# Differential-attention scores on two row halves of TensorE, with a smaller PSUM ring

## The chip, the core and the metric

The kernel runs on one core of a Trainium2 chip. The metric is device time in microseconds (us) of one execution of the whole kernel; lower is better. The engines named below are TensorE (PE; its weight loads are listed apart as PEld), VectorE (DVE), ScalarE (ACT), GpSimd (POOL) and SyncE (SP, which issues most DMAs).

## The reference, cut to what matters

One layer of a diffusion trunk: a SwiGLU feed-forward, then token mixing (differential attention beside a bidirectional mLSTM), then a second feed-forward, each behind a modulated normalization. 512 latent tokens read themselves and 256 cached context keys; 128 prompt tokens read only themselves. The change lies in the attention:

```
scale = DA_HEAD_DIM ** -0.5                      # 64 features, 8 heads, 2 components
def block(qi):                                   # 128 queries
    s = jnp.einsum('bqhcd,bkhcd->bhcqk', qi, kf) * scale
    pr = jax.nn.softmax(s, axis=-1)
    w = pr[:, :, 0] - lam * pr[:, :, 1]
    return jnp.einsum('bhqk,bkhv->bqhv', w, vf)
```

So each head has two components of 64 features; each has its own scores and its own softmax, and the two weight matrices are subtracted before they meet the values.

## The kernel before, in words

**Precision by parts.** Most products are made from numbers split into a high part that the fp32r format holds (a ScalarE copy) and the rest (a VectorE subtraction). A product is the sum of high x high, high x low and low x high (`mm3`).

**Stages.** First the modulation, with products on four column quarters of the array (`product`, line 905, `tile_position=(0, q)`) between the first feed-forward's products; then that feed-forward. Then the attention's pools open at line 1346: `ps2`, a ring of five one-bank PSUM tiles, and `ps2s`, one three-bank tile for scores. In these pools run:

- the first projections (lines 1833 to 1850): `tok_group` makes query tokens 0 and 1, then key tokens 0 and 1 of the first head pair, then query tokens 2, 3, 4, then key tokens 2, 3, 4. Each group takes one bank per token tile of 128, and `norm2(psum, 1)`, called inside the first group, takes one for the norm's sums. ScalarE copies a finished bank into `q_tok` or `k_tok`. The gates' small products go into the score tile (`ps_g`);
- the branch gates (`Gates`, line 1793), with accumulators from `ps2`;
- the attention, head by head, mixed with projection units for later heads and for the mLSTM (`Fill`).

**One head.** `pack_queries` writes per token and component the high part, the low part, the low part and the high part of the other component in four slots of 64; `pack_keys` writes each component's high part twice. `queries`, `keys(0)` and `keys(1)` turn these through TensorE (ten 128x128 transposes each, names `qpk`, `kpk`, `kp`) into tiles with features on the rows: `qT` has for each component its high part on one half of the rows and its low part on the other, `kH` has the high keys twice, `kL` the low keys twice. So one 128-row product of `qT` with `kH` adds high x high and low x high, and one with `kL` adds the rest and low x low. The cached keys come doubled from memory (`cache_kd`).

`scores(qi)` makes for each component 768 columns of scores, in blocks of 512 and 256 that keep inside a PSUM bank: eight matmuls into the three-bank tile. For the prompt's queries (`qi` = 4) four matmuls of 256 columns stand in two banks. VectorE takes a minimum over both components, ScalarE makes two exponentials with sums (`soft`), VectorE mixes them (`mix`), TensorE turns the weights (`turn`, up to six 128x128 transposes, read by ScalarE) and multiplies by the values (`values`, f32, names `ps_o`).

**The order.** TensorE's and SP's instructions keep the order of the code. Inside `with written()` VectorE's and ScalarE's do too; elsewhere a scheduler places them. For each query block the code writes scores, the turning of the block before, exponentials, one projection unit, the mix, the values of the block before, and a second unit where the table `UNITS` (line 1930) says so; heads 6 and 7 have one unit per block, and the queries of head 7 are prepared with no unit between. A unit is 24 matmuls: `ps_t` (token rows, 256 columns) or `ps_p` (feature rows, 320 columns). `gate_rows` (line 1366) is a long chain of small VectorE steps that the scheduler lays between the first head's preparations.

Of the kernel before, what the change touches and what calls it, by code (L numbers as in the profile page):

```python
# [31 lines left out]
def tile_trunk(ctx: ExitStack, tc: tile.TileContext, a: dict):  # L32
    nc = tc.nc
    vec = nc.vector
# [15 lines left out]
    def act(*args, **kw):  # L50
        return placed(nc.scalar.activation(*args, **kw))  # L51

    def tt(eng, out, in0, in1, op):
        return placed(eng.tensor_tensor(out=out, in0=in0, in1=in1, op=op))  # L54
# [19 lines left out]
    def mm(*args, **kw):  # L74
        tc.keep_in_program_order(nc.tensor.matmul(*args, **kw))  # L75
# [32 lines left out]
    ntmp = right.enter_context(tc.tile_pool(name="ntmp", bufs=1, side="right"))  # L108
# [721 lines left out]
    with ExitStack() as ph:  # L830
        fp = ph.enter_context(tc.tile_pool(name="ffn1", bufs=1))
        psum = Banks(ph.enter_context(tc.tile_pool(name="ps1", bufs=1, space=PSUM)))
# [7 lines left out]
        hs = HalfStep(1, fp, ntmp, psum, a["w1a"], a["w3a"], a["w2a"], range(*FIRST_GROUPS[1]))  # L840
# [130 lines left out]
        start = Opening()  # L971
# [371 lines left out]

    att = ExitStack()
    qk = att.enter_context(tc.tile_pool(name="qk", bufs=1))
    psum = att.enter_context(tc.tile_pool(name="ps2", bufs=5, space=PSUM))
    ps_s = att.enter_context(tc.tile_pool(name="ps2s", bufs=1, space=PSUM))

    fill = Fill()
# [2 lines left out]
    def gate_products():  # L1352
        raw = load(rawp, [128, KT, 128], a["w_g"], tag="raw", name="wg_raw")
        wgH = wide_p.tile([128, KT, 128], F32R, tag="BH", name="wgH", bufs=2)
        wgL = wide_p.tile([128, KT, 128], F32R, tag="BL", name="wgL", bufs=2)
        act(wgH, raw, AF.Copy)
        tt(vec, wgL, raw, wgH.bitcast(F32), ALU.subtract)
        ps = ps_s.tile([128, 1536], F32, tag="sc", name="ps_g")

        def step(hf, k):  # L1360
            cs = half(hf)
            mm3(ps[:, 512 * hf : 512 * hf + HALF], wgH[:, k, :], wgL[:, k, :], hH[:, k, cs], hL[:, k, cs], k == 0, k == KT - 1)

        return ps, step
# [125 lines left out]
    q_tok, k_tok, v_tok = {}, {}, {}  # L1490
# [49 lines left out]
    class Head:  # L1540
# [8 lines left out]

        def pack_queries(self):  # L1550

            hs = slice(self.h * 128, (self.h + 1) * 128)
            qv = q_tok[self.pr][:, :, hs].rearrange("p t (c d) -> p t c d", c=2)
            self.qpk = ap.tile([128, 5, 4, 64], F32R, tag="pk", name="qpk", bufs=2)
            act(self.qpk[:, :, 0::3, :], qv, AF.Copy)
            tt(vec, self.qpk[:, :, 1:3, :], qv, self.qpk[:, :, 0::3, :].bitcast(F32), ALU.subtract)

        def pack_keys(self):
            hs = slice(self.h * 128, (self.h + 1) * 128)
            kv = self.kv = k_tok[self.pr][:, :, hs].rearrange("p t (c d) -> p t c d", c=2)  # L1560
            self.kpk = ap.tile([128, 5, 4, 64], F32R, tag="pk", name="kpk", bufs=2)
            for i in range(2):
                self.at_act = act(self.kpk[:, :, i::2, :], kv, AF.Copy)

        def turn_features(self, pk, dst, key, ev):
            for i0, n in ((0, 2), (2, 2), (4, 1)):
# [7 lines left out]

        def queries(self):
            self.qT = ap.tile([128, 2, T], F32R, tag="qT", name="qT")
            self.kH = ap.tile([128, 2, 896], F32R, tag="kH", name="kH")
            self.kL = ap.tile([128, 2, 896], F32R, tag="kL", name="kL")
            self.ao = ap.tile([128, 5, 128], F32, tag="ao", name="ao")
            self.turn_features(self.qpk, self.qT, False, lambda o, i: act(o, i, AF.Copy))  # L1580
            self.kp2 = ap.tile([128, 5, 4, 64], F32R, tag="pk", name="kp2", bufs=2)
            for i in range(2):
                self.at_vec = tt(vec, self.kp2[:, :, i::2, :], self.kv, self.kpk[:, :, i::2, :].bitcast(F32), ALU.subtract)
            ck = load(ap, [128, 2, 256], a["cache_kd"][:, self.hd], tag="asq", name="ck")
            act(self.kH[:, :, 512:768], ck, AF.Copy)
            tt(vec, self.kL[:, :, 512:768], ck, self.kH[:, :, 512:768].bitcast(F32), ALU.subtract)

        def keys(self, part):
            if part == 0:
                self.turn_features(self.kpk, self.kH, True, lambda o, i: vec.tensor_copy(o, i))  # L1590
            else:
                self.turn_features(self.kp2, self.kL, True, lambda o, i: act(o, i, AF.Copy))

        def scores(self, qi):
            s = ps_s.tile([128, 1536], F32, tag="sc", name="sc")
            qs = slice(qi * 128, (qi + 1) * 128)
            qT, kH, kL = self.qT, self.kH, self.kL
            for c in range(2):
                if qi < 4:
                    for k0, k1 in (((0, 512), (512, 768)) if c == 0 else ((0, 256), (256, 768))):  # L1600
                        o = s[:, c * 768 + k0 : c * 768 + k1]
                        mm(o, qT[:, c, qs], kH[:, c, k0:k1], start=True, stop=False)
                        mm(o, qT[:, c, qs], kL[:, c, k0:k1], start=False, stop=True)
                else:

                    o = s[:, c * 512 : c * 512 + 256].rearrange("p (c t) -> p c t", c=2)
                    mm(o, qT[:, c, qs], kH[:, :, 768:896], start=True, stop=False)
                    mm(o, qT[:, c, qs], kL[:, :, 768:896], start=False, stop=True)
            if qi < 4:
                sv = s.rearrange("p (c t) -> p c t", c=2)  # L1610
            else:
                sv = s[:, 0:1280].rearrange("p (c t) -> p c t", c=2)[:, :, 0:128]
            mn, sm, rc = (ap.tile([128, 2], F32, tag=n, name=n, bufs=2) for n in ("mn", "sm", "rc"))
            placed(vec.tensor_reduce(out=mn, in_=sv, axis=AX.X, op=ALU.min))
            self.s[qi] = sv, 768 if qi < 4 else 128, mn, sm, rc
# [201 lines left out]
    ropes, tabs, nlam, gs, rope_p = [], [], [None], [None], [None]  # L1817
    wide = ExitStack()
    wide_p = wide.enter_context(tc.tile_pool(name="wide", bufs=1))
    G = Gates(wide_p, ntmp, psum)  # L1820

    (src_q, e_q), (src_k, e_k) = project_q(0, ropes.append), project_k(0, ropes.append)
    e_q, e_k = e_q(), e_k()
# [11 lines left out]
    with tc.issue_after(box["normed"]):  # L1835
        ps_g, gate_step = gate_products()
# [63 lines left out]
    ap = att.enter_context(tc.tile_pool(name="att", bufs=1, reuse_waits="tile"))  # L1900
# [36 lines left out]
    for hd in range(8):  # L1937
        H = heads[hd]
        odd = hd % 2
        for qi in range(5):  # L1940
            n = UNITS[hd][qi]
# [24 lines left out]
        n = UNITS[hd][-1]  # L1966
# [40 lines left out]
    psum = ml.enter_context(tc.tile_pool(name="ps3", bufs=8, space=PSUM, reuse_waits="tile"))  # L2007
# [238 lines left out]
    psum = Banks(ctx.enter_context(tc.tile_pool(name="ps4", bufs=1, space=PSUM, reuse_waits="tile")))  # L2246
# [67 lines left out]
    hs = HalfStep(2, None, tmp, psum, a["w1b"], a["w3b"], a["w2b"], range(GROUPS[0][0], FB))  # L2314
# [45 lines left out]
    ps = {(f, i): acc_tile(psum) for f in range(2) for i in range(2)}  # L2360
# [9 lines left out]
    ps = {(f, i): acc_tile(psum) for f in range(2) for i in range(2)}  # L2370
# [169 lines left out]
```

## Time and profile before

| what | us |
|---|---|
| median of 3 runs | 1818.51 (1817.56 to 1819.2) |
| span of the profiled execution | 1816.4 |
| TensorE busy in it | 1793.6 (99%) |
| VectorE busy | 1323.8 (73%) |
| ScalarE busy | 894.8 (49%) |

The span runs from the first to the last instruction of the profiled execution; what lies around it (launch and end) is not in it. Matmuls overlap in the timeline: a row's duration runs from its start to its modelled end, and the next matmul begins before that. What a matmul costs in a row of matmuls is therefore the distance between starts. A column with a tile such as 128*128 gives rows and columns of the array that the instruction uses. A bracket at a row's end gives idle time of the engine just before it and what ended it.

### The profile page before, as it was taken

How to read it: one execution, taken by the hardware profiler on the slowest of the kernel's cores; microseconds unless marked ns; L12 is line 12 of the kernel's file. 1: busy time of each engine (PE TensorE's matmuls, PEld its weight loads, DVE VectorE, ACT ScalarE, POOL GpSimd, SP SyncE). 2: the span in 40 equal slices, each digit the busy share in tenths (PEclk: the TensorE clock that was granted, in tenths of full speed). 3: DMA queues.
4: the chain of work that ended last, by engine and by line, in shares of the span. 5: the costliest groups of instructions: out<-in, count | busy, mean ns of one | idle time of the engine just before them, and what ended most of it. 6: DMA issues, size and time to landing. Idle time of an engine off the chain costs nothing.

```text
span 1816.4 us, 30813 instructions
## 1 busy us (share of the span) xinstructions
PE 1793.6 (99%) x12622; PEld 1754.8 (97%) x12622; DVE 1323.8 (73%) x2140; ACT 894.8 (49%) x1558; POOL 37.1 (2%) x65
## 2 busy tenths in 40 slices
PE   9999999999999999999999999999999999999998
PEld 7999999999999999999999889999999999999998
DVE  6889986677886776475575649876767888897485
ACT  5654553333755454455465454674336545554432
POOL 0000000100000000000000000000000000000010
PEclk9999999999999999999999999999999999999999
DMA  8255566977244322112222055665652355657992
GB/s 330 106 197 183 185 224 235 344 228 257 82 138 159 106 76 78 63 63 89 80 89 72 20 169 163 223 254 183 238 170 80 134 172 185 202 181 275 352 307 83
DMA packets 130622, 307.69 MB, mean 169 GB/s; under 512 B 9841, under 2 KB 92017, under 8 KB 117553
## 3 DMA queue, kind: packets, MB, share of 16 engines
q1 hardware_dynamic: 120114, 263.64, 42.1%
q0 software_dynamic: 9680, 39.46, 6.7%
q8 instruction: 99, 1.62, 0.4%
q10 hardware_dynamic: 688, 2.63, 0.4%
q14 instruction: 41, 0.34, 0.1%
HBM read 238.14 MB, written 67.56 MB: 168 GB/s over the span
## 4 chain that ended last, share of the span: by engine, by line
PE 84%; DVE 7%; DMA 5%; ACT 3%; issue 1%; SPq 0%; DVEq 0%; ACTq 0%
PE ps_f L75 43%; PE ps_p L75 19%; PE ps_t L75 11%; PE sc L75 3%; PE ps_o L75 2%; DVE ww L54 2%; PE ps_n L75 2%; DMA raw<-in_w2b 2%; DMA raw_a<-in_w_ada_k 1%; PE ps_wT L78 1%; PE ps_u L75 1%; DVE junk L813 1%; PE ps_qkT L78 1%; DMA out_new_c<-Cn 1%; DMA P<-nm_dram 1%
## 5 line engine op out<-in xcount | busy, mean ns | idle before, releaser
L75 PE MATMUL ps_f<-S,ww 128*128 128x320 f32 x2184 | 352.5, 310 | 3.0 <-DMA S<-g_dram 1.0
L75 PEld LDWEIGHTS ps_f<-S,ww 128*128 128x128 f32 x2184 | 327.5, 188 | 7.0 <-DVE ww L54 4.6
L75 PE MATMUL ps_p<-hH,wH 128*128 128x320 f32 x672 | 212.4, 316 | 0.7 <-DVE stage L61 0.7
L75 PE MATMUL ps_p<-hH,wL 128*128 128x320 f32 x672 | 207.7, 309 | 0.0
L75 PE MATMUL ps_p<-hL,wH 128*128 128x320 f32 x672 | 207.7, 309 | 0.0
L54 DVE TENSOR_TENSOR ww<-raw,ww 128x2048 fp32r<-128x2048 f32 (+1 forms) x67 | 150.2, 2241 | 63.7 <-ACT ww L51 63.6
L75 PE MATMUL ps_f<-hm,ww 128*128 128x320 f32 x1176 | 185.8, 309 | 0.6 <-DVE ww L54 0.6
L75 PE MATMUL ps_t<-wH,hH 128*128 128x256 f32 x640 | 185.2, 289 | 0.9 <-DVE x L57 0.9
L75 PE MATMUL ps_t<-wH,hL 128*128 128x256 f32 x640 | 181.0, 283 | 0.9 <-DVE hL L54 0.9
L75 PE MATMUL ps_t<-wL,hH 128*128 128x256 f32 x640 | 180.8, 283 | 0.0
L75 PEld LDWEIGHTS ps_f<-hm,ww 128*128 128x128 f32 x1176 | 175.7, 188 | 1.2 <-DVE ww L54 1.2
L75 PE MATMUL ps_f<-hm,wB 128*128 128x320 f32 x1008 | 161.5, 309 | 0.0
L51 ACT ACTIVATE ww<-raw 128x2048 fp32r<-128x2048 f32 (+1 forms) x67 | 125.3, 1871 | 57.9 <-DVE raw L54 33.6
L75 PEld LDWEIGHTS ps_f<-hm,wB 128*128 128x128 f32 x1008 | 151.3, 188 | 0.0
L54 DVE TENSOR_TENSOR raw<-raw 128x1024 f32<-128x1024 f32 x168 | 145.3, 865 | 1.9
L75 PEld LDWEIGHTS ps_p<-hH,wH 128*128 128x128 f32 x672 | 126.4, 188 | 1.2 <-DVE stage L61 0.9
L75 PEld LDWEIGHTS ps_p<-hL,wH 128*128 128x128 f32 x672 | 126.3, 188 | 0.3
L75 PEld LDWEIGHTS ps_p<-hH,wL 128*128 128x128 f32 x672 | 126.2, 188 | 0.0
L51 ACT ACTIVATE u<-ps_f 128x320 f32<-128x320 f32 x117 | 50.7, 433 | 153.2 <-PE ps_f L75 153.1
L75 PEld LDWEIGHTS ps_t<-wH,hH 128*128 128x128 f32 x640 | 122.3, 191 | 1.5 <-ACT nsq L51 1.1
L75 PEld LDWEIGHTS ps_t<-wH,hL 128*128 128x128 f32 x640 | 122.3, 191 | 1.1 <-DVE hL L54 1.1
L75 PEld LDWEIGHTS ps_t<-wL,hH 128*128 128x128 f32 x640 | 122.5, 191 | 0.4
(307 smaller groups left out, 3444.8 us busy)
## 6 DMA issues: line engine op xcount, KB each, us to landing
g_dram<-g SPq DMA_DIRECT2D x44, 640.0 KB, 7.5
raw_a<-in_w_ada_c POOLq DMA_DIRECT2D x31, 512.0 KB, 4.7
g_dram<-g SPq DMA_DIRECT2D x24, 480.0 KB, 8.2
raw<-in_w1b SPq DMA_DIRECT2D x11, 1024.0 KB, 4.8
raw<-in_w3b SPq DMA_DIRECT2D x11, 1024.0 KB, 6.3
raw<-in_w1a SPq DMA_DIRECT2D x10, 1024.0 KB, 4.9
raw<-in_w3a SPq DMA_DIRECT2D x10, 1024.0 KB, 6.5
hm<-g_dram SPq DMA_DIRECT2D x7, 1280.0 KB, 13.3
```

Source lines behind the costliest of these rows:

```text
L51: return placed(nc.scalar.activation(*args, **kw))
L54: return placed(eng.tensor_tensor(out=out, in0=in0, in1=in1, op=op))
L75: tc.keep_in_program_order(nc.tensor.matmul(*args, **kw))
L78: tc.keep_in_program_order(nc.tensor.transpose(*args, **kw))
L813: placed(vec.tensor_tensor_reduce(out=junk, in0=raw, in1=self.csil[:, v, :], op0=ALU.mult, op1=ALU.add, scale=1.0, scalar=0.0, accum_out=m ...
```

## The change

The scores of the two components are laid on the two halves of the array's rows. `queries` and `keys` now pack high parts of both components in two slots and low parts in the other two (one helper, `both`), so that after the transposes rows 0 to 63 hold component 0 and rows 64 to 127 component 1, once for the high part (`[:, 0]`) and once for the low part (`[:, 1]`). Keys are held once, in one tile `kT`; the third set of transposes (`kp2`) goes, and the cached keys are loaded once in two 64-row DMAs. Each block of scores is three 64-row products per component, with `tile_position` (0, 0) and (64, 0) in turn. The two components' scores stand 1024 columns apart, so the score tile takes four banks and the ring four instead of five. In the gates stage a small class, `Five`, puts every fifth accumulator into the third bank of the score tile.

```
-    psum = att.enter_context(tc.tile_pool(name="ps2", bufs=5, space=PSUM))
+    psum = att.enter_context(tc.tile_pool(name="ps2", bufs=4, space=PSUM))
...
-        ps = ps_s.tile([128, 1536], F32, tag="sc", name="ps_g")
+        ps = ps_s.tile([128, 2048], F32, tag="sc", name="ps_g")
...
         def pack_queries(self):
 
+            self.qpk = self.both(q_tok, "qpk")
+
+        def both(self, of, name):
             hs = slice(self.h * 128, (self.h + 1) * 128)
-            qv = q_tok[self.pr][:, :, hs].rearrange("p t (c d) -> p t c d", c=2)
-            self.qpk = ap.tile([128, 5, 4, 64], F32R, tag="pk", name="qpk", bufs=2)
-            act(self.qpk[:, :, 0::3, :], qv, AF.Copy)
-            tt(vec, self.qpk[:, :, 1:3, :], qv, self.qpk[:, :, 0::3, :].bitcast(F32), ALU.subtract)
+            v = of[self.pr][:, :, hs].rearrange("p t (c d) -> p t c d", c=2)
+            pk = ap.tile([128, 5, 4, 64], F32R, tag="pk", name=name, bufs=2)
+            self.at_act = act(pk[:, :, 0:2, :], v, AF.Copy)
+            self.at_vec = tt(vec, pk[:, :, 2:4, :], v, pk[:, :, 0:2, :].bitcast(F32), ALU.subtract)
+            return pk
 
         def pack_keys(self):
-            hs = slice(self.h * 128, (self.h + 1) * 128)
-            kv = self.kv = k_tok[self.pr][:, :, hs].rearrange("p t (c d) -> p t c d", c=2)
-            self.kpk = ap.tile([128, 5, 4, 64], F32R, tag="pk", name="kpk", bufs=2)
-            for i in range(2):
-                self.at_act = act(self.kpk[:, :, i::2, :], kv, AF.Copy)
+            self.kpk = self.both(k_tok, "kpk")
...
-            self.kp2 = ap.tile([128, 5, 4, 64], F32R, tag="pk", name="kp2", bufs=2)
-            for i in range(2):
-                self.at_vec = tt(vec, self.kp2[:, :, i::2, :], self.kv, self.kpk[:, :, i::2, :].bitcast(F32), ALU.subtract)
-            ck = load(ap, [128, 2, 256], a["cache_kd"][:, self.hd], tag="asq", name="ck")
-            act(self.kH[:, :, 512:768], ck, AF.Copy)
-            tt(vec, self.kL[:, :, 512:768], ck, self.kH[:, :, 512:768].bitcast(F32), ALU.subtract)
+            ck = ap.tile([128, 256], F32, tag="asq", name="ck")
+            for c in range(2):
+                dma(ck[64 * c : 64 * c + 64], a["cache_kd"][64 * c : 64 * c + 64, self.hd, c])
+            act(self.kT[:, 0, 512:768], ck, AF.Copy)
+            tt(vec, self.kT[:, 1, 512:768], ck, self.kT[:, 0, 512:768].bitcast(F32), ALU.subtract)
 
         def keys(self, part):
             if part == 0:
-                self.turn_features(self.kpk, self.kH, True, lambda o, i: vec.tensor_copy(o, i))
-            else:
-                self.turn_features(self.kp2, self.kL, True, lambda o, i: act(o, i, AF.Copy))
+                self.turn_features(self.kpk, self.kT, True, lambda o, i: vec.tensor_copy(o, i))
 
         def scores(self, qi):
-            s = ps_s.tile([128, 1536], F32, tag="sc", name="sc")
+            s = ps_s.tile([128, 2, 1024], F32, tag="sc", name="sc")
...
-            for c in range(2):
-                if qi < 4:
-                    for k0, k1 in (((0, 512), (512, 768)) if c == 0 else ((0, 256), (256, 768))):
-                        o = s[:, c * 768 + k0 : c * 768 + k1]
-                        mm(o, qT[:, c, qs], kH[:, c, k0:k1], start=True, stop=False)
-                        mm(o, qT[:, c, qs], kL[:, c, k0:k1], start=False, stop=True)
...
+            blocks = ((0, 512), (512, 768)) if qi < 4 else ((640, 896),)
+            for k0, k1 in blocks:
+                for n, (i, j) in enumerate(((0, 0), (0, 1), (1, 0))):
+                    for c in range(2):
+                        r = slice(64 * c, 64 * c + 64)
+                        mm(
+                            s[:, c, k0 - blocks[0][0] : k1 - blocks[0][0]], self.qT[r, i, qs], self.kT[r, j, k0:k1],
+                            start=n == 0, stop=n == 2, tile_position=(64 * c, 0),
+                        )
+            sv = s[:, :, 0:768] if qi < 4 else s[:, :, 128:256]
...
-    G = Gates(wide_p, ntmp, psum)
+    class Five:
...
+        def tile(self, shape, dtype, tag, name):
+            self.n += 1
+            return psum.tile(shape, dtype, tag=tag, name=name) if self.n % 5 else ps_g[:, 1024:1536]
+
+    G = Gates(wide_p, ntmp, Five())
```

More of the change, by code (lines that the diff above doesn't have):

```diff
@@ L1576, in queries @@
             self.qT = ap.tile([128, 2, T], F32R, tag="qT", name="qT")
-            self.kH = ap.tile([128, 2, 896], F32R, tag="kH", name="kH")
-            self.kL = ap.tile([128, 2, 896], F32R, tag="kL", name="kL")
+            self.kT = ap.tile([128, 2, 896], F32R, tag="kT", name="kT")
             self.ao = ap.tile([128, 5, 128], F32, tag="ao", name="ao")
             self.turn_features(self.qpk, self.qT, False, lambda o, i: act(o, i, AF.Copy))
-            self.kp2 = ap.tile([128, 5, 4, 64], F32R, tag="pk", name="kp2", bufs=2)
@@ L1594, in scores @@
         def scores(self, qi):
-            s = ps_s.tile([128, 1536], F32, tag="sc", name="sc")
+            s = ps_s.tile([128, 2, 1024], F32, tag="sc", name="sc")
             qs = slice(qi * 128, (qi + 1) * 128)
-            qT, kH, kL = self.qT, self.kH, self.kL
-            for c in range(2):
-                if qi < 4:
-                    for k0, k1 in (((0, 512), (512, 768)) if c == 0 else ((0, 256), (256, 768))):
-                        o = s[:, c * 768 + k0 : c * 768 + k1]
-                        mm(o, qT[:, c, qs], kH[:, c, k0:k1], start=True, stop=False)
-                        mm(o, qT[:, c, qs], kL[:, c, k0:k1], start=False, stop=True)
[L1604 to L1612, printed above, removed]
+            blocks = ((0, 512), (512, 768)) if qi < 4 else ((640, 896),)
[7 more added lines that the diff above has]
+                        )
@@ L1819, in tile_trunk, with __init__ @@
     wide_p = wide.enter_context(tc.tile_pool(name="wide", bufs=1))
-    G = Gates(wide_p, ntmp, psum)
+    class Five:
+        def __init__(self):
+            self.n = 0
+        def tile(self, shape, dtype, tag, name):
+            self.n += 1
+            return psum.tile(shape, dtype, tag=tag, name=name) if self.n % 5 else ps_g[:, 1024:1536]
+    G = Gates(wide_p, ntmp, Five())
     (src_q, e_q), (src_k, e_k) = project_q(0, ropes.append), project_k(0, ropes.append)
```

## Prediction

> **What bounds the kernel now.** I read the busy times of the page first, then one stretch of the windows, then the timeline of TensorE. The page gives the span and each engine's busy time; the third row is the window of the attention stage (length, then busy time of PE, PEld, DVE, ACT and POOL, clock, DMA share, GB/s).
>
> ```profile
> span 1816.4 us, 30813 instructions
> PE 1793.6 (99%) x12622; PEld 1754.8 (97%) x12622; DVE 1323.8 (73%) x2140; ACT 894.8 (49%) x1558; POOL 37.1 (2%) x65
> 607.00:1036.00 429.00, 425.68 (x3371) 416.39 (x3370) 262.29 (x399) 226.45 (x468) 0.00 (x0) 1.00 0.22 74
> ```
>
> TensorE is the bound: it idles 3.3 us of the 429 us in which the change works. So whatever TensorE no longer does comes off the end, whatever it newly waits for is added, and work removed from VectorE and ScalarE is worth nothing by itself. The span, 1816.4 us, lies 2.1 us below the median of the runs, 1818.5 us; I add the sum to the median. A measurement of this kernel tells about 0.2%, 3.6 us, from no change.
>
> One block of scores (128 queries, both components), from the timeline of TensorE; columns are start, duration, instruction, output and inputs, array tile, shape:
>
> ```profile
> 805.09 0.39 PE L75 MATMUL sc<-kH,qT 128*128 128x512 f32 x1
> 805.32 0.39 PE L75 MATMUL sc<-kL,qT 128*128 128x512 f32 x1
> 805.55 0.28 PE L75 MATMUL sc<-kH,qT 128*128 128x256 f32 x1
> 805.67 0.28 PE L75 MATMUL sc<-kL,qT 128*128 128x256 f32 x1
> 805.79 0.28 PE L75 MATMUL sc<-kH,qT 128*128 128x256 f32 x1
> ...
> 806.50 0.82 PE L78 MATMUL ps_wT<-ident,p 128*128 128x128 f32 x6
> ```
>
> Durations overlap, so the price is the distance of starts: 0.231 us at 512 columns, 0.118 at 256. The block costs 4 x 0.231 + 4 x 0.118 = 1.40, as 806.50 - 805.09 shows.
>
> **The change, part 1: the scores.** The order of TensorE at the second query block of the first head, before: a projection (ps_t), then the scores (sc), each against high keys and low keys (kH, kL).
>
> ```order
> L75 MATMUL ps_t<-wL,hH 128x256
> L75 MATMUL ps_t<-wH,hL 128x256
> L75 MATMUL sc<-kH,qT 128x512
> L75 MATMUL sc<-kL,qT 128x512
> L75 MATMUL sc<-kH,qT 128x256
> L75 MATMUL sc<-kL,qT 128x256
> ```
>
> The second component follows with the same four. Now, with keys in one tile (kT):
>
> ```order
> L75 MATMUL ps_t<-wL,hH 128x256
> L75 MATMUL ps_t<-wH,hL 128x256
> L75 MATMUL sc<-kT,qT 128x512 x6
> L75 MATMUL sc<-kT,qT 128x256 x6
> L78 MATMUL ps_wT<-ident,p_6235 128x128 x6
> ```
>
> Eight matmuls of 128 rows became twelve of 64 rows, in six pairs, one of each pair on rows 0-63, the other on 64-127. If a pair runs side by side it costs one matmul, if not, two: 3 x 0.231 + 3 x 0.118 = 1.05, or 2.09. No row here shows row halves. The nearest are the modulation's products at the start of the kernel, which stand on four column quarters (128*32):
>
> ```profile
> 25.50 0.31 PE L75 MATMUL ps_f<-hm,wH 128*128 128x320 f32 x1
> 25.74 1.07 PE L75 MATMUL ps_a<-raw_a,small 128*32 128x256 f32 x16
> 26.74 0.42 PE L75 MATMUL ps_f<-hm,wH 128*128 128x320 f32 x1
> 26.99 0.46 PE L75 MATMUL ps_f<-hm,wH 128*128 128x320 f32 x2
> 25.74 0.59 PEld L75 LDWEIGHTS ps_a<-raw_a,small 128*32 128x32 f32 x16 [0.19 <-issue]
> ```
>
> Sixteen instructions take 1.00 us, 0.0625 each, half of what a 256-column matmul costs alone above though each f32 product here is two instructions. Tiles do run side by side, so I take one matmul per pair.
>
> The same rows price the change of tile shape. An ordinary 320-column matmul spaces 0.147 (3.52 / 24, below), so the array was free at 25.65, but the first ps_a load starts at 25.74: 0.09 us idle. On the way out the first ps_f starts at 26.74 and the next at 26.99, 0.25 instead of 0.147: its weight load, 0.10 us, lay open. A full load costs 1.25 / 12 = 0.104 us where loads set the pace:
>
> ```profile
> 800.24 1.50 PE L75 MATMUL ps_o<-v_tok,wT 128*128 128x128 f32 x12
> 801.49 0.39 PE L75 MATMUL ps_p<-hH,wH 128*128 128x320 f32 x1
> 801.73 3.52 PE ps_p L75 x24
> ```
>
> So a switch costs about 0.09 + 0.104 = 0.195 us, two per block 0.39. [...]
>
> New block: 1.05 + 0.39 = 1.44, against 1.40, x 32 = +1.1 us. The prompt's block (one per head) had four 256-column matmuls, 0.47, and gets three pairs, 0.36 + 0.39 = 0.75, x 8 = +2.2. Where scores follow f32 products their first load lay open already:
>
> ```profile
> 821.71 0.36 PE L75 MATMUL sc<-kH,qT 128*128 128x256 f32 x1
> 821.91 0.28 PE L75 MATMUL sc<-kL,qT 128*128 128x256 f32 x1
> ```
>
> 0.20 instead of 0.118; ten blocks stand so by the unit table, -0.8. Part 1: **+2.5 us**. The quarter of products saved is eaten by eighty switches.
>
> **Part 2: the keys' transposes.** The order of TensorE at the last head, before (kp is the low part of the keys), then now:
>
> ```order
> L78 MATMUL ps_qkT<-identr,qpk 128x128 x10
> L75 MATMUL ps_o<-v_tok,wT 128x128
> L78 MATMUL ps_qkT<-identr,kpk 128x128 x10
> L78 MATMUL ps_qkT<-identr,kp_10739 128x128 x10
> L75 MATMUL sc<-kH,qT 128x512
> ```
> ```order
> L78 MATMUL ps_qkT<-identr,qpk 128x128 x10
> L75 MATMUL ps_o<-v_tok,wT 128x128
> L78 MATMUL ps_qkT<-identr,kpk 128x128 x10
> L75 MATMUL sc<-kT,qT 128x512 x6
> L75 MATMUL sc<-kT,qT 128x256 x6
> ```
>
> Ten transposes per head go.
>
> ```profile
> 834.59 0.81 PE ps_qkT L78 x10
> 828.38 0.35 PE L75 MATMUL ps_t<-wH,hH 128*128 128x256 f32 x1
> 828.57 0.28 PE L75 MATMUL ps_t<-wL,hH 128*128 128x256 f32 x1
> 1000.02 1.13 PE L78 MATMUL ps_qkT<-identr,kp 128*128 128x128 f32 x10 [0.64 <-DVE kp L54]
> 1001.39 0.50 PE L75 MATMUL sc<-kH,qT 128*128 128x512 f32 x1 [0.23 <-DVE kH L1590]
> ```
>
> 0.81 us in the chain, and 0.07 more because the matmul behind a transpose spaces 0.19 instead of 0.118: 0.88 x 7 heads = 6.2. In the last head no projection stands between; the queue waited 0.64 and 0.23 there, and the scores will wait for the keys' copies instead; I give it 0.8. Part 2: **-7.0 us**.
>
> Their copies, splits and half the cached-key bytes go too, and SP issues two small loads for one. All of it lies under TensorE's 99%: nothing; bare, a late cached key would cost a block's wait, under 1 us.
>
> **Part 3: four PSUM banks in the ring instead of five.** A bank must now be read out four allocations later, not five. In the gates stage the new helper puts every fifth accumulator into the score tile, so five rotate as before: nothing. Elsewhere I took each bank's read-out end in the trace and the start of the product four allocations on. Most have room; these don't.
>
> ```profile
> 480.34 0.28 PE L75 MATMUL ps_t<-wH,hL 128*128 128x256 f32 x1
> 480.46 0.28 PE L75 MATMUL ps_t<-wH,hH 128*128 128x256 f32 x1
> 481.41 1.75 ACT L51 ACTIVATE hH<-x,mod,scale 128x192 fp32r<-128x192 f32 x4
> 483.06 0.63 ACT L51 ACTIVATE k_tok<-ps_t 128x256 f32<-128x256 f32 x2
> 653.97 0.35 PE L75 MATMUL ps_t<-wH,hH 128*128 128x256 f32 x1
> 653.53 1.91 ACT L51 ACTIVATE wH<-raw 128x2048 fp32r<-128x2048 f32 x1
> 655.33 0.27 ACT L51 ACTIVATE wT<-ps_wT 128x128 f32<-128x128 f32 x1
> 775.92 0.35 PE L75 MATMUL ps_t<-wH,hH 128*128 128x256 f32 x1
> 777.27 0.27 ACT L51 ACTIVATE wT<-ps_wT 128x128 f32<-128x128 f32 x1
> ```
>
> First, in the projections ahead of the gates: allocations run q, q, the norm's sums, k, k, q, q, q. The third q of the last group takes the bank of the first k, which ScalarE reads at 483.06, behind the second half's normalization, until about 483.4; the product starts at 480.46. All following products are queued behind it: +3.0 us, and nothing later in that stage waits, so nothing gives it back. Second and third, between heads 0 and 1 and between 2 and 3: the projection behind the queries' transposes takes the bank of the last weights' transpose, read only at 655.60, since ScalarE splits a weight first: 655.60 - 653.97 = 1.63, and 777.54 - 775.92 = 1.62; +3.2 us.
>
> Fourth, at the first head VectorE's order moves. Before, then now (b, lf, Ml are gate rows; the CASTs free the keys' banks):
>
> ```order
> L1398 MEMSET lf_6170 64x640
> L1590 CAST kH_5984<-ps_qkT_6063 128x2x256
> L1411 COPY bl_6461<-b_6172 32x5
> L1590 CAST kH_5984<-ps_qkT_6069 128x2x256
> L1590 CAST kH_5984<-ps_qkT_6075 128x2x128
> ```
> ```order
> L1406 SCALAR_TENSOR_TENSOR lf_6148<-keep_6149,m0_6139,u_6151 4x512 x2
> L1410 COPY Ml_6450<-lf_6148 32x5
> L1411 COPY Ml_6450<-lf_6148 32x5
> L1588 CAST kT_5981<-ps_qkT_6057 128x2x256
> L61 TENSOR_SCALAR fg_6141<-lf_6148 64x640
> ```
>
> The copies stand behind the last scans, and the second projection behind them needs the first copy's bank.
>
> ```profile
> 596.85 0.61 DVE L1590 CAST kH<-ps_qkT 128x512 fp32r<-128x512 f32 x1
> 603.12 2.58 DVE L1406 TENSOR_TENSOR_SCAN lf<-keep,m,u 4x512 f32<-4x512 f32 x2
> 603.14 0.41 PE L75 MATMUL ps_p<-hH,wH 128*128 128x320 f32 x1 [0.72 <-DVE stage L61]
> ```
>
> The 2.58 us of scans moved ahead, the split that leaves lets the rows begin earlier, and the old wait of 0.72 goes: between -0.7 and +2 us, I take +0.7. Waits under 0.3 us at other places add about 0.4. Part 3: **+7.3 us**, between +5 and +9.
>
> Sum: 2.5 - 7.0 + 7.3 = +2.8, with an old wait of 0.2 us gone at each of two heads +2.4. 1818.5 + 2.4 = **1821 us**, +0.13%, inside what counts as no change; with +-3 us on it, it is as often just above.
>
> **The rivals.**
>
> Row tiles switch without emptying the array. Part 1 becomes 32 x (1.05 - 1.40) + 8 x (0.36 - 0.47) = -12.1 instead of +2.5: 1806 us. For it: no row here shows a switch to row halves, and ps_a's is one of columns. Against: both ends of the ps_a group show the idle and the open load. If only one part of the price is paid, the time lies between, 1806 to 1821. Together 0.22.
>
> The two weight loads of a pair run one after the other. A load is 0.104, two 0.208: 512-column pairs hide that (0.231), 256-column ones don't (0.118), so it decides wherever two loads outlast one product: 3 x 0.09 + 0.10 at the entry = +0.37 a block, x 40 = +15 us: 1836 us, slower. For it: each load still brings 128 columns. Against: sixteen ps_a loads took 0.59 us, but they are 32 columns each. 0.11.
>
> The halves don't run side by side. Every block has six more matmuls, 32 x 1.05 + 8 x 0.36 = +36.5: 1858 us; the change then doesn't do what it says. For it: no row shows row halves. Against: ps_a. 0.12.
>
> Loads don't hide inside the tiled stretch: six loads of 0.104 open per block, three in the prompt's, 32 x 0.62 + 8 x 0.31 = +22: 1844 us. Against: the sixteen ps_a products would not fit in 1.00 us with open loads. 0.04. [...]
>
> **How the numbers follow.** Forecast 0.51; rivals 0.22, 0.11, 0.12, 0.04. The range takes the forecast, the faster rival and the slower 1836: 1805 to 1838, leaving 0.16 outside; the forecast's own range is 1817 to 1825. Of the forecast's 0.51, 0.27 lies within 0.2%, 0.04 below and 0.20 above; of the first rival, 0.20 is faster and 0.02 the same. Faster 0.24, same 0.29, slower 0.47.
>
> **What would show it.** In the new profile: pairs starting a few ns apart, 0.23 and 0.12 between pairs (else the third or second rival); 0.09 us and an open load before and behind every block (else the first); a wait of 3 us at 480 and of 1.6 us behind two heads' query transposes (else part 3); one group of ten transposes fewer per head. Blocks of 1.1 us or of 2.1 us would make the prediction wrong, and so would missing bank waits.

## The result, and the profile after

The changed kernel takes 1823.5 us in the median of nine runs (1820.2 to 1825.4), against 1818.6 us for the kernel before (1816.1 to 1820.1): a ratio of 1.0026, with a 95% interval of 1.0016 to 1.0036. It is slower by 4.9 us. A second measurement on another chip (the last experiment below) gave 1821.7 against 1818.9 us, 1.0017 [1.0008, 1.0025]. The forecast was 1821.0 with a range of 1805 to 1838; slower by more than 0.2% had 0.47.

The page of the profile after gives the span and the busy times; below it stand three windows of before and three of after (length, busy time and count of PE, PEld, DVE, ACT and POOL, then the granted clock, the DMA share and GB/s). They cover the projections and gates, the preparation of the first head, and the attention.

```profile
span 1821.7 us, 30918 instructions
PE 1792.9 (98%) x12686; PEld 1745.1 (96%) x12686; DVE 1315.4 (72%) x2132; ACT 881.2 (48%) x1526; POOL 37.3 (2%) x65
```
```profile
100.00:500.00 400.00, 395.32 (x2709) 391.04 (x2709) 319.40 (x458) 185.61 (x280) 16.63 (x28) 1.00 0.63 213
500.00:610.00 110.00, 109.28 (x780) 109.14 (x779) 85.79 (x126) 54.52 (x86) 0.00 (x0) 1.00 0.41 141
610.00:1040.00 430.00, 426.68 (x3379) 417.39 (x3378) 261.27 (x396) 226.38 (x469) 0.00 (x0) 1.00 0.22 73
```
```profile
100.00:500.00 400.00, 392.01 (x2662) 387.47 (x2661) 319.84 (x459) 185.06 (x278) 16.70 (x28) 0.99 0.63 213
500.00:610.00 110.00, 107.92 (x769) 107.38 (x769) 80.21 (x117) 51.73 (x81) 0.00 (x0) 1.00 0.37 125
610.00:1040.00 430.00, 424.71 (x3458) 407.17 (x3458) 257.23 (x392) 214.40 (x441) 0.00 (x0) 1.00 0.22 75
```

TensorE idles more in each: 7.99 instead of 4.68 us, 2.08 instead of 0.72, 5.29 instead of 3.32. That is 6.6 us of new waiting. In the first window the granted clock is no longer 1.00.

The score block at the place shown of before, then the way out of another block (the same columns as there):

```profile
804.87 0.28 PE L75 MATMUL ps_t<-wH,hL 128*128 128x256 f32 x1
805.08 1.31 PE L75 MATMUL sc<-kT,qT 64*128 64x512 f32 x12
806.32 0.55 PE L78 MATMUL ps_wT<-ident,p 128*128 128x128 f32 x3
...
857.11 1.31 PE L75 MATMUL sc<-kT,qT 64*128 64x512 f32 x12
858.35 0.39 PE L75 MATMUL ps_t<-wH,hH 128*128 128x256 f32 x1
858.58 0.28 PE L75 MATMUL ps_t<-wL,hH 128*128 128x256 f32 x1
```

Twelve products take 1.24 us from start to start. If the halves went one after the other they would need 6 x 0.231 + 6 x 0.118 = 2.09, so they run side by side. The array was free at 804.87 + 0.118 = 804.99 and the first product starts at 805.08: 0.09 us idle, as in the row of column tiles. Inside the 1.24 us lie 1.05 of work, 0.10 of the first open load and again 0.09 of idleness at the end. Behind a block, the first projection spaces 0.23 instead of 0.118: 0.11 of open load.

The waits, from the list of the waits of TensorE in 480 to 1040 us (total, times, longest):

```profile
PE ps_t L75 <- ACT wT L51: 3.1, 2, 1.5
PE ps_t L75 <- ACT k_tok L51: 2.9, 1, 2.9
PE ps_p L75 <- DVE kT L1588: 1.0, 1, 1.0
...
PE sc L75 <- DVE kT L1588: 0.7, 1, 0.7
```

The first three are what the shorter ring was expected to bring: 2.86 us in the first projections, 1.53 us twice between heads, and the first head's keys. The timeline around the 2.86 us shows what was not expected:

```profile
481.09 0.28 PE L75 MATMUL ps_t<-wL,hH 128*128 128x256 f32 x1
481.21 0.28 PE L75 MATMUL ps_t<-wH,hL 128*128 128x256 f32 x1
484.34 0.58 PE L75 MATMUL ps_t<-wH,hH 128*128 128x256 f32 x1 [2.86 <-ACT k_tok L51]
...
485.15 0.41 PE L75 MATMUL ps_t<-wH,hH 128*128 128x256 f32 x1
485.37 0.41 PE L75 MATMUL ps_t<-wL,hH 128*128 128x256 f32 x1
```

Ahead of the wait the same product spaces 0.12 us, behind it 0.21. Windows over this place, before and then after, and last the one behind the first wait of 1.53 us:

```profile
480.00:503.00 23.00, 23.00 (x183) 23.00 (x184) 21.86 (x33) 13.46 (x25) 0.00 (x0) 1.00 0.13 47
```
```profile
480.00:503.00 23.00, 19.39 (x138) 19.19 (x139) 22.95 (x34) 12.96 (x23) 0.00 (x0) 0.85 0.13 46
660.00:670.00 10.00, 8.47 (x64) 8.33 (x64) 5.40 (x7) 5.90 (x10) 0.00 (x0) 0.83 0.32 107
```

A mean clock of 0.85 over 23 us is 6.9 us at half speed; 0.83 over 10 us is 3.4 us. (The trace's own record of the granted clock has 0.5 from 483.33 to 490.16 and from 664.24 to 667.65 us.) A 256-column product costs 0.213 instead of 0.118 us there, so 45% of such a stretch is lost: 3.0 and 1.5 us, 4.5 together. The second wait of 1.53 us, at 787 us, has no such stretch behind it in this profile.

So the account of the profile is: scores +0.8, transposes -7.0 (both counted from rows, as worked out below), waits +6.6, half clock +4.5, in sum +4.9. The spans differ by 5.3. The account leaves out the first 100 us, where TensorE idles 0.6 us more than before, and the stages behind 1040 us, where it idles 1.2 us less.

### The profile page after: what moved, and what is told of

It reads as the page before. It is cut to its first block, busy times and chain, and to the rows that moved or that the text cites. A ratio compares the mean times of both kernels' runs of the same rounds, so it can differ in the third digit from the quotient of the medians.

```text
span 1821.7 us, 30918 instructions
## 1 busy us (share of the span) xinstructions
PE 1792.9 (98%) x12686; PEld 1745.1 (96%) x12686; DVE 1315.4 (72%) x2132; ACT 881.2 (48%) x1526; POOL 37.3 (2%) x65
## 4 chain that ended last, share of the span: by engine, by line
PE 84%; DVE 6%; DMA 5%; ACT 3%; issue 1%; SPq 0%; DVEq 0%; ACTq 0%
PE ps_f L75 41%; PE ps_p L75 19%; PE ps_t L75 11%; PE ps_o L75 2%; PE sc L75 2%; PE ps_n L75 2%; DVE ww L54 2%; DMA raw<-in_w2b 2%; PE ps_wT L78 1%; DMA raw_a<-in_w_ada_k 1%; DMA P<-nm_dram 1%; PE ps_u L75 1%; PE ps_g L75 1%; DVE junk L813 1%; ACT hH L51 1%
## 5 line engine op out<-in xcount | busy, mean ns | idle before, releaser
L75 PE MATMUL ps_f<-S,ww 128*128 128x320 f32 x2148 | 346.8, 310 | 3.4 <-DMA S<-g_dram 1.1
L75 PEld LDWEIGHTS ps_f<-S,ww 128*128 128x128 f32 x2148 | 322.1, 188 | 7.4 <-DVE ww L54 4.8
L54 DVE TENSOR_TENSOR wL<-raw,wH 128x2048 fp32r<-128x2048 f32 x43 | 98.3, 2285 | 38.1 <-ACT wH L51 38.0
```

## The experiments

My theory after the result: the score blocks cost what they did, and what the shorter ring makes TensorE wait, with the half clock behind these waits, is all that turns a gain of 6 us into a loss of 5. The rival: the 64-row blocks cost more than their rows show, or slow what stands beside them, and taking the waits away gives little. The ratios below are against runs of the kernel before on the same chip.

**The first wait alone.** The third query tile of the group takes a bank of the score tile that nobody uses yet.

```
-    def tok_group(psum, jobs, between):
+    def tok_group(psum, jobs, between, spare=()):
-        ps = [psum.tile([128, 512], F32, tag="mm", name="ps_t")[:, :256] for _ in jobs]
+        ps = [psum.tile([128, 512], F32, tag="mm", name="ps_t")[:, :256] for _ in jobs[len(spare):]]
+        ps += spare
...
-    tok_group(psum, [(w_q, i, e_q) for i in (2, 3, 4)], lambda k: None)
+    tok_group(psum, [(w_q, i, e_q) for i in (2, 3, 4)], lambda k: None, [ps_g[:, 1536:1792]])
```

> The changed kernel with one difference: in the first projections the bank of the third query tile comes from an unused column range of the four-bank score tile, so the product need not wait for ScalarE to read the first key bank. Theory A (the bank wait at 484 us costs its own 2.9 us and, since TensorE stands still so long, the halved clock that follows costs about 2.9 us more, 5.8 us of products at half speed): TensorE idles no 2.9 us there, the granted clock stays 1.00 from 480 to 503 us, and the time falls by 5 to 6 us against the changed kernel, to about 1818, level with the kernel before. Theory B (only the wait counts; the half clock has another cause): it falls by 2.9 us, to about 1820.6, and the clock still dips there. Theory C (the wait is given back later in the stage): no change, 1823.5.

Measured: 1817.0 us (1814.5 to 1819.0), ratio 0.9990 [0.9981, 0.9999]. One bank is worth 6.5 us against the changed kernel's 1823.5 (4.7 against its second median), though the wait was 2.86. The mean of the granted clock over the runs rises with it, from 0.9976 to 0.9991: 5.5 us less at half speed, 2.5 us of loss, which with the wait makes 5.3. The windows of this kernel show why, and a second thing:

```profile
480.00:503.00 23.00, 22.08 (x178) 21.88 (x177) 21.86 (x38) 14.38 (x29) 0.00 (x0) 1.00 0.13 47
780.00:800.00 20.00, 18.51 (x145) 18.11 (x146) 15.40 (x25) 10.32 (x22) 0.00 (x0) 0.91 0.16 60
```

With the wait the half clock at 480 us is gone. The two waits of 1.53 us are still there, and now the second has 20 x 0.09 / 0.5 = 3.6 us of half clock behind it and the first none: which of the two is hit differs from profile to profile.

**The two waits between heads.** VectorE reads the prompt's turned weights instead of ScalarE, which has a weight to split at that time.

```
-                act(wT[:, k0 : k0 + n, :], p[:, :n, :], AF.Copy)
+                if qi == 4 and self.hd < 7:
+                    placed(vec.tensor_copy(wT[:, k0 : k0 + n, :], p[:, :n, :]))
+                else:
+                    act(wT[:, k0 : k0 + n, :], p[:, :n, :], AF.Copy)
```

> The changed kernel with one difference: the last weights' transpose of a head (prompt queries, heads 0 to 6) is read out by VectorE, not by ScalarE behind a 1.9 us weight split. Theory A (the two waits of 1.53 us between heads 0 and 1 and between heads 2 and 3 are bank waits on that read-out, and the first brings 3.4 us of half clock, 1.7 us of work): both waits vanish, the clock stays 1.00 from 650 to 665 us, and the time falls by 3.1 to 4.8 us against the changed kernel, to about 1819 to 1820.5. Theory B (the projection there waits for something else, such as the weights): the waits stay and the time stays at 1823.5.

Measured: 1818.9 us (1815.5 to 1823.4), ratio 1.0000 [0.9990, 1.0011], 4.6 us under the changed kernel. Each wait of 1.53 us becomes one of 0.33, on the queries' copies; the wait at 480 us stays with its half clock:

```profile
PE ps_t L75 <- ACT k_tok L51: 2.9, 1, 2.9
...
PE ps_qkT L78 <- ACT qT L51: 0.7, 2, 0.3
```

Two waits shortened by 2.4 us and one stretch of half clock, 1.5 us, make 3.9 of the 4.6.

**All three places of the ring.** Both edits above, and ScalarE instead of VectorE copies the first head's turned keys, so that they don't stand behind the gate rows' scans.

```
-                self.turn_features(self.kpk, self.kT, True, lambda o, i: vec.tensor_copy(o, i))
+                self.turn_features(self.kpk, self.kT, True, (lambda o, i: act(o, i, AF.Copy)) if self.hd == 0 else (lambda o, i: vec.tensor_copy(o, i)))
```

> The changed kernel with both differences of the two runs above, and the first head's turned keys copied by ScalarE, not by VectorE behind the gate rows. If the ring of four is all that makes the change lose (theory A), every large wait of TensorE in the projections and the attention is gone (idle from 464 to 1036 us back to about that of the kernel before, 6 us), the granted clock stays 1.00 to the end, and what is left is the gain of the turned keys less the cost of the switches: 10 to 11.5 us under the changed kernel, about 1812 to 1813.5, so 5 to 6 us under the kernel before. If the switches of the array's tiling are the larger loss (rival, part 1 at +2.5 us or more), it stays at 1815 or above.

Measured: 1813.4 us (1809.8 to 1814.9), ratio 0.9965 [0.9953, 0.9978]. This beats both kernels. By the account it should lie 7.0 - 0.8 - 0.4 = 5.8 us under the kernel before (0.4 is what TensorE idles more in the three windows), and by the medians it lies 5.9 under it. In the window of the first head's preparation TensorE's idleness falls from 2.08 to 1.23 us; in the attention it is 3.06, less than before the change:

```profile
500.00:610.00 110.00, 108.77 (x771) 108.48 (x770) 83.55 (x122) 54.61 (x87) 0.00 (x0) 1.00 0.41 140
610.00:1040.00 430.00, 426.94 (x3484) 409.31 (x3483) 259.45 (x400) 212.67 (x434) 0.00 (x0) 1.00 0.21 71
```

**The ring alone.** The kernel before, with four banks in the ring, the four-bank score tile and the gates' fifth accumulator in it. Scores and transposes are as they were.

```
-    psum = att.enter_context(tc.tile_pool(name="ps2", bufs=5, space=PSUM))
+    psum = att.enter_context(tc.tile_pool(name="ps2", bufs=4, space=PSUM))
...
-        ps = ps_s.tile([128, 1536], F32, tag="sc", name="ps_g")
+        ps = ps_s.tile([128, 2048], F32, tag="sc", name="ps_g")
...
-    G = Gates(wide_p, ntmp, psum)
+    G = Gates(wide_p, ntmp, Five())
```

> The kernel before with the ring cut alone: four banks in the ring, four in the score tile (the fourth unused by the scores), every fifth accumulator of the gates stage in the score tile, as in the change; scores, keys and transposes as before. Theory A: the same waits appear as in the changed kernel, about 2.9 us at 484 us with half clock behind it, 1.5 us between heads 0 and 1 and between heads 2 and 3, so +7 us of waits and 3 to 5 us of half clock: 1826 to 1830, clearly slower than the kernel before, and slower than the whole change. Rival (the ring cut is harmless, the loss is in the scores): 1818.6, as before.

Measured: 1830.6 us (1829.6 to 1832.3), ratio 1.0065 [1.0052, 1.0078], 11.3 us above the kernel before by the medians. The missing bank alone costs more than twice what the whole change does. Its waits, and its windows of less than full clock:

```profile
PE ps_t L75 <- ACT wT L51: 3.0, 2, 1.5
PE ps_t L75 <- ACT k_tok L51: 2.9, 1, 2.9
...
PE ps_qkT L78 <- DVE stage L61: 0.9, 1, 0.9
PE ps_p L75 <- ACT kL L51: 0.6, 1, 0.6
```
```profile
480.00:500.00 20.00, 16.95 (x126) 16.74 (x127) 19.97 (x33) 12.07 (x21) 0.00 (x0) 0.91 0.15 53
660.00:680.00 20.00, 18.48 (x145) 18.20 (x144) 17.45 (x27) 11.74 (x25) 0.00 (x0) 0.91 0.18 61
1000.00:1020.00 20.00, 19.33 (x137) 18.33 (x136) 13.65 (x25) 12.06 (x29) 0.00 (x0) 0.91 0.14 53
```

New waits of 2.9 + 3.0 + 0.9 + 0.6 = 7.4 us and three stretches of half clock of 3.4 us, 1.5 each, make 11.9.

**The transposes alone.** The kernel before, without the ten transposes of the low parts per head; their tile is filled with copies of the high parts, so the scores lack the low part of the new keys.

```
...
-                self.turn_features(self.kp2, self.kL, True, lambda o, i: act(o, i, AF.Copy))
...
+                act(self.kL[:, :, 0:512], self.kH[:, :, 0:512].bitcast(F32), AF.Copy)
+                act(self.kL[:, :, 768:896], self.kH[:, :, 768:896].bitcast(F32), AF.Copy)
```

> The kernel before without the second turning of the keys through TensorE: the low parts of the new keys are not made, ScalarE copies the turned high parts into their place, so the two differ only in what the scores of new keys add up. Eighty transposes fewer; ring, score tile and products as before. Theory (part 2 of the prediction): 7.0 us less than the kernel before, since TensorE is the bound there and 0.88 us per head comes off, and no new wait of TensorE over 0.5 us. Rival: the scores then wait for the copies in every head and less than half of it comes off, 3 us or less.

Measured: 1814.6 us (1811.0 to 1815.2), ratio 0.9967 [0.9954, 0.9979], which is 3.8 to 8.4 us less (4.3 by the medians; two of the five runs lie near 1811, three near 1815). That no new wait above 0.5 us would come did not hold: in its last head the scores now wait for the copies that the turning had hidden:

```profile
996.20 0.80 PE L75 MATMUL sc<-kH,qT 128*128 128x512 f32 x1 [2.00 <-DVE kH L1591]
997.29 0.79 PE L75 MATMUL sc<-kL,qT 128*128 128x512 f32 x1 [0.29 <-ACT kL L51]
997.88 0.41 PE L75 MATMUL sc<-kH,qT 128*128 128x256 f32 x1
998.10 0.41 PE L75 MATMUL sc<-kL,qT 128*128 128x256 f32 x1
```

The 2.0 us replace 0.9 of before, and half clock follows again (0.22 us from product to product at 256 columns). In the changed kernel, where the scores read only one copied tile, that wait is 0.65 us, and no half clock follows it.

**Two visits to the row halves per block.** From the kernel of all three edits on: between the 512-column and the 256-column products the block before is turned, so that 24 of the 40 blocks switch tile shape four times instead of twice.

```
+                if k0 != 512:
+                    middle()
...
-                H.scores(qi)
-                if qi > 0:
-                    H.turn(qi - 1)
+                H.scores(qi, (lambda: H.turn(qi - 1)) if qi > 0 else (lambda: None))
```

> On the version with all three waits removed (e3_all, 1813.4 us): the turning of the block before is put between the 512-column and the 256-column pairs of a score block, in 24 of the 40 blocks, so TensorE changes between full rows and row halves twice more in each; the work is the same. Theory (a switch costs about 0.09 us of empty array and 0.06 to 0.11 us of open weight load): +0.31 us a block, +7.4 us, to 1819 to 1823, part of the excess from softmax waits in the last two heads. Rival (a switch costs only what the trace shows as the load, or is hidden behind the reads of the results): +0 to +3 us.

Measured: 1822.8 us (1821.8 to 1824.3), ratio 1.0020 [1.0010, 1.0029], 9.3 us above the kernel that it was made from (10.0 by the two ratios, since the two ran on different chips). A switch costs what the rows show: two more per block and 24 blocks give 48 switches at 0.195 us, 9.4 by the prediction's price; the trace gives a part of the 9.3 to longer waits of the turning for the mixed weights `p`, 2.1 us in sum instead of 0.7.

```profile
PE ps_wT L78 <- DVE p L57: 2.1, 5, 0.5
```
```profile
PE ps_wT L78 <- DVE p L57: 0.7, 4, 0.2
```

That leaves 7.9 us, 0.16 per switch. (First this kernel's row, then that of the kernel it was made from.)

**The halves apart in the queue.** From the kernel of all three edits on: first component 0's three products, then component 1's three.

```
-                for n, (i, j) in enumerate(((0, 0), (0, 1), (1, 0))):
-                    for c in range(2):
-                        r = slice(64 * c, 64 * c + 64)
+                for c in range(2):
+                    r = slice(64 * c, 64 * c + 64)
+                    for n, (i, j) in enumerate(((0, 0), (0, 1), (1, 0))):
```

> On the same version (e3_all, 1813.4 us): the same twelve matmuls of a score block in another order, three of component 0, then three of component 1, for each column range. Theory (two row halves run side by side only when neighbours in the queue, because products start in the order of the program): five slots for six products, +0.48 us a block and +0.24 us for the prompt's, +17 us, to about 1830. Rival (the array fills the free half with a later product by itself): no change.

Measured: 1811.9 us (1810.6 to 1812.8), ratio 0.9958 [0.9945, 0.9972]. The theory that the two products of a pair have to be neighbours in the queue falls. The block costs no more than with the products in turn, 785.70 to 786.95, 1.25 us (the second fence is the answer for 785.69 to 785.72 alone: both halves have started by then):

```profile
785.70 1.32 PE L75 MATMUL sc<-kT,qT 64*128 64x512 f32 x12
786.95 0.39 PE L75 MATMUL ps_t<-wH,hH 128*128 128x256 f32 x1
```
```profile
785.70 0.51 PE L75 MATMUL sc<-kT,qT 64*128 64x512 f32 x2
```

In the program the second half's first product stands behind three of the first half's, and yet starts within 17 ns of the first of them: the answer that ends at 785.712 holds both, from 785.70 on (3 ns apart, 805.077 and 805.080, where they stand in turn in the changed kernel). The rows do not name the half, but two 512-column products this close are not of one half, which would space them 0.23 us. Whether this order is even the better one stays open: the two kernels' times overlap.

**The wait filled.** All of the above leave open whether it is the idleness that halves the clock. This kernel keeps the bank and its lateness, but gives TensorE 23 products that nobody reads.

```
...
+                if cover is not None and k == 0 and i == 4:
+                    for _ in range(23):
+                        mm(cover, hH[:, 0, 0:128], wh[:, 0:256], start=True, stop=True)
                 mm3(p, hH[:, k, tok], hL[:, k, tok], wh[:, k * 256 : (k + 1) * 256], wl[:, k * 256 : (k + 1) * 256], k == 0, k == KT - 1)
```

> The changed kernel, with 23 products of 128x256 that nobody reads (into the fourth bank of the score tile, from operands already there) in front of the product that waited 2.86 us for its bank. They take 23 x 0.118 = 2.71 us, so the product starts when it did, but TensorE does not idle before it. What they compute goes nowhere. If it is the idleness that halves the clock: granted clock 1.00 in 480 to 503 us, 27 products at 0.118 instead of 0.213 us, about 2.6 us less than the changed kernel, which is run beside it: 1820 to 1821.5. If the half clock belongs to the place or to the bank: 0.85 there and no difference. The two waits of 1.53 us stay in either case, with or without a stretch of half clock behind one of them.

The unaltered changed kernel beside it:

> The changed kernel once more, unaltered, as the yardstick for the filled wait on the same chip: 1823 to 1824, with the wait of 2.86 us and a granted clock of about 0.85 in 480 to 503 us. If the half clock behind a wait of 1.53 us is a matter of chance, this profile may show it behind the first, the second or neither.

Measured: 1818.4 us (1816.8 to 1820.7), ratio 0.9996 [0.9987, 1.0005], against 1821.7 us (1819.4 to 1824.5), 1.0017 [1.0008, 1.0025], for the unaltered one: 3.3 us less for work that goes nowhere. (Both came out about 2 us under what was expected.) The mean granted clock of the eleven runs each is 0.9993 and 0.9977, which is 5.6 us less at half speed, or 2.5 us. First the filled kernel's timeline and window, then the unaltered kernel's two windows:

```profile
481.79 2.92 PE L75 MATMUL ps_g<-wH,hH 128*128 128x256 f32 x23
484.81 0.39 PE L75 MATMUL ps_t<-wH,hH 128*128 128x256 f32 x1
485.03 0.28 PE L75 MATMUL ps_t<-wL,hH 128*128 128x256 f32 x1
485.15 0.28 PE L75 MATMUL ps_t<-wH,hL 128*128 128x256 f32 x1
```
```profile
480.00:503.00 23.00, 21.97 (x178) 21.53 (x177) 22.96 (x36) 14.67 (x28) 0.00 (x0) 1.00 0.14 47
```
```profile
480.00:503.00 23.00, 19.90 (x145) 19.70 (x146) 22.97 (x35) 13.30 (x25) 0.00 (x0) 0.85 0.14 46
786.00:793.00 7.00, 7.00 (x51) 7.00 (x51) 5.60 (x9) 3.34 (x7) 0.00 (x0) 0.77 0.47 152
```

The bank still comes 3 us late (481.79 to 484.81), but the clock stays at 1.00 and the products behind it space 0.12. So it is the idle time that halves the clock, not the place. In the unaltered kernel the second wait of 1.53 us, not the first, is followed by half clock this time: 7 x 0.23 / 0.5 = 3.2 us.

Not tried: scores of both components in three banks with a ring of five, where the two halves would write one bank at the same time; no run here shows what that does.

## Why the prediction came out as it did

The sum was +2.4 us, the measurement +4.9 and, repeated, +2.8. The mechanism was the one forecast; its terms, in turn.

**Scores: +2.5 forecast, about +0.8.** Pairs cost one product (twelve take 1.24 us, not 2.09), and a switch leaves the array idle for 0.09 us: both as the ps_a rows had it. The size was off at the way out. A load of 0.104 was to lie open there; ahead of the projections it does (0.11), ahead of the weights' transposes only 0.05 does (six of them span 0.87 us instead of 0.82):

```profile
652.24 0.28 PE L75 MATMUL ps_t<-wH,hL 128*128 128x256 f32 x1
652.44 0.62 PE L75 MATMUL sc<-kT,qT 64*128 64x256 f32 x6
653.00 0.87 PE L78 MATMUL ps_wT<-ident,p 128*128 128x128 f32 x6
```

Transposes stand behind 32 of the 40 blocks, and behind them a full block costs 0.09 + 1.24 + 0.05 = 1.38 instead of 1.44, the prompt's (653.00 - 652.24 - 0.118 + 0.05) 0.69 instead of 0.75. Against 1.40 and 0.47 that is 24 x -0.02 + 8 x 0.04 + 8 x 0.22 = +1.6, less the forecast's 0.8 for the ten blocks behind f32 products, which no row here measures anew.

The idle time is 0.09 us at each edge of a tiled stretch, now for row tiles too.

**Transposes: -7.0 forecast.** The groups of ten went as counted, one per head, and alone they are worth 6.0 [3.8, 8.4] us with a new wait of 2.0 in the last head. In the changed kernel that wait is 0.65 instead of 0.64 + 0.23. The step holds within that interval, and the -7.0 stays in the account as counted.

**Ring: +7.3 forecast, +6.6 of waits measured.** Place by place: 3.0 forecast and 2.86 found; 1.63 and 1.62, and 1.53 twice; at the first head +0.7, and 2.08 - 0.72 = +1.4, the upper part of the range given. The -0.4 for two old waits came true as well: neither is in the list of waits.

**What the sum lacked: the half clock, +4.5 us in that profile, about +2 on average.** The prediction's step "+3.0 us, and nothing later in that stage waits, so nothing gives it back" counted a wait at its length. It costs its length and then up to as much again, since TensorE comes out of it at half speed: 3.3 us by the filled wait. With it the terms give 0.8 - 7.0 + 6.6 + 4.5 = +4.9 for the profiled run. That this is also the difference of the medians is chance: over all runs the granted clock averages 0.9976 in the 20 of the changed kernel and 0.9989 in 57 of the kernel before, 4.5 us more at half speed, or +2.0. With that the terms give +2.4, near the repeated +2.8, and what is left of the first +4.9 stays open. The profile of before could not show it, since none of its waits in the stages that the change touches is longer than 1 us and its clock there is 1.00 throughout. The forecast came out near partly by luck: this missing term and the scores' 1.7 us too much have opposite signs; and its range left room.

**The rivals.** Row tiles switch without emptying: no, 0.09 us lies idle at each edge, and doubling the switches cost 9.3 us. The loads of a pair one after the other, or open inside the stretch: no, 1.24 us leaves no room for six more loads of 0.104; behind the first pair, each pair's loads are for the rows in use and cost nothing inside it. Halves one after the other: no, that would be 2.09.

**What the change is worth.** With its three waits taken away it gains 0.35% [0.22, 0.47]; by the account that is the transposes. The row halves as such, three 64-row products per component instead of two of 128 rows, bring nothing by that account (+0.8): eighty switches eat the quarter of the products that they save. No run had the row halves alone.

## What to carry to other kernels

Before a PSUM buffer is taken from a ring, read for each of its tiles when the reader ends and when the product that many allocations later starts; each negative distance is a wait. Three of the four could be read here to a tenth of a microsecond, not the one at the first head, where VectorE's order changed. Where TensorE is the bound, charge a wait above 1.5 us up to double (here 2.86 us brought 1.5 or 3.0 us more at half clock, 1.53 us 1.5 in four cases of ten), and prefer to move the late reader to another engine or borrow an idle bank: three such edits turned +0.26% into -0.35%. Row halves pay 0.16 to 0.2 us per switch, twice a visit, so by these prices they are worth it where many tiled products stand together, not in blocks of a microsecond.

## What the hardware showed that was not expected

**Short waits halve the clock, some of the time.** Over the eleven profiles from 475 to 1760 us, by their lists of waits and their clock in windows of 20 us: all four waits of 2.86 us and the one of 2.0 us have half clock behind them, of twelve waits of 1.5 to 1.8 us five do. In the first 40 us, where TensorE waits for the modulation's weights, the changed kernel's two waits of 1.72 and 1.73 us have none behind them. Not every profile is at full clock outside 100 to 1760 us: the one without the transposes has a mean clock of 0.996, where its one stretch of 6.8 us in these windows would leave 0.998. A stretch lasts 3.4 or 6.8 us (3.41 and 6.82 in the changed kernel). One stretch, in the kernel with the ring alone, lies between 1010 and 1020 us, and from 1000 to 1020 us TensorE idles only 0.67 us in all, so length is not all of it.

The traces' record of the clock shows part of the rest. In the changed kernel every change falls on a whole multiple of 3.413 us after 5.46 us, where the record first gives full clock: 483.33 is 140 such slots later, 490.16 is 142, 664.24 is 193 and 667.65 is 194. In the kernel before, whose record begins with full clock at 6.41 us, the one change, at 1815.47 us, is 530 slots later, behind the last product. Adding up TensorE's idleness slot by slot in these two up to the last product, of the slots at full clock those of the changed kernel with 2.68 us (from 479.91) and 1.53 us (from 660.82) are followed by half clock; its two of 1.72 and 1.69 us in the first 40 us, one of 1.40 us in the kernel before and all with less are not. A wait that a border cuts seems to count in parts: the one at 787 us, cut 1.22 to 0.31, was not hit. What decides among these was not tried. A slot need not be idle throughout: 1.53 us of idleness was enough at 660.82, and 1.72 was not at 8.88.

**A product for the free half of the rows overtakes.** With three products of one half queued ahead of those of the other, the other half's first starts within 17 ns of the first of the three, and the blocks cost the same 1.25 us. These rows, with the 1811.9 us, speak against products of two row halves starting strictly in the order of the program.
